# Keeping the activations of the last 16 expert blocks in SBUF between the hidden stage and the values stage

## The chip, the cores and the metric

One core of one Trainium2 chip runs the kernel. The metric is the device time of one execution in microseconds; the time before is the median of three runs. A profile is one execution recorded by the hardware profiler.

## The reference

A hybrid encoder layer is applied to a prompt of 512 tokens and a sample of 256 tokens: RMSNorm, one input projection, two attention mixers, the output projection with a residual, and then PEER, a layer of 128 x 128 = 16384 single-neuron experts. Only PEER matters here:

```python
def peer(h, w_q, sub_keys, u, v):
    ...
        best, pos = lax.top_k(cand, PEER_TOPK)
        eidx = jnp.take_along_axis(cand_idx, pos, axis=-1)
        g = jax.nn.softmax(best, axis=-1)
        act = jax.nn.gelu(jnp.einsum('cd,cpkd->cpk', xc, u[eidx]).astype(jnp.float32), approximate=False)
        return jnp.einsum('cpk,cpkd->cd', (g * act).astype(xc.dtype), v[eidx])
```

Each token picks 8 x 16 = 128 experts. Expert e contributes its gate times GELU(x . u[e]) times the row v[e].

## The kernel before

The 256 sample tokens fetch their experts by indirect DMA on POOL (`row`, L738: 128 rows of u and v, 1 MB, 256 of them), with the dot product and the sum on DVE (L740, L748). This goes on from the routing of the sample to nearly the end, beside everything else, paced by `early`, a list that names for each pair of dots the weight split after which they stand in DVE's order.

The 512 prompt tokens are done densely: all 16384 experts, in 128 blocks of 128, with a gate that is zero where a token did not pick an expert. Three stages do that.

*Hidden*: for block j, `hidden` (L601) loads 128 rows of u (`raw`, 0.5 MB, on SP), splits them into a high and a low part (`hi` on ACT, L72; `lo` on DVE, L73), runs 24 matmuls of 512 columns (`pu`, three for each of 8 chunks, L67 to L69), takes the GELU on ACT (`ge`, L608) and writes 256 KB to the DRAM tensor `h_d` (L609, issued by ACT). `raw` has three buffers. The first 16 blocks fill gaps of the routing; the others come after the gates in the program, but in fact run beside them.

*Gates*: one-hot matmuls (`pg`, L666) build the gate of each expert and token in 16 pieces (`gb`, 2 MB each), which are written to the DRAM tensor `g_d` (L670). Their pools, `gm` and `rq`, take much of SBUF, and are closed (`left.close()`, `rqx.close()`) behind the hidden loop.

*Values*: the pool `dense` (`dp`, 64 KB of each partition) is opened then, in the room that the gates had. For each pair of blocks jp, SP loads the hidden activations (`gw` from `h_d`, L699, three buffers) and for every fourth pair the gates of 8 blocks (`gblk` from `g_d`, L685, 2 MB, two buffers). DVE multiplies the two in place (L701), ACT and DVE split the product into `w` (which takes the buffers of `x2p`, the hidden matmuls' operand), the rows of v come as `raw` and are split like those of u, and 48 matmuls add to the 8 PSUM banks `py`. After the second pair the residual is loaded (`x1y`, four loads of 512 KB on SP, L712) and added through 64 matmuls with an identity (L715). At the end `py` is copied out.

Each engine runs its instructions in a fixed order, and so does each DMA queue. That order is worked out when the kernel is built, by a planner that goes by the order of the program, but takes a later instruction ahead where an earlier one isn't ready by its own timing. So a load of the values stage can stand in SP's queue among loads of the hidden stage, as soon as a buffer for it is free.

Of the kernel before, what the change touches and what calls it, by code (L numbers as in the profile page):

```python
# [11 lines left out]
F32 = mybir.dt.float32  # L12
F32R = mybir.dt.float32r
U32 = mybir.dt.uint32
BF = mybir.dt.bfloat16
AF = mybir.ActivationFunctionType
# [5 lines left out]
P = 128  # L22
D = 1024
# [7 lines left out]
NK = 128  # L31
# [7 lines left out]
DENSE = 4  # L39
# [5 lines left out]
NCAND = 64  # L45
FIRST_GATHER = 36
FILL = 16
NOSYNC = mybir.DependencyInfo(mybir.DependencyClass.NoSync, mybir.DependencyReason.DATA)


@with_exitstack
def tile_kernel(ctx, tc, xs_in, relb, onehot, logm, g1, w_in, gqk, lamv, gdiff, w_out, g2,
                w_q, skT, uT, uv, out_p, out_s, dbg=None):
    nc = tc.nc
    V, S, G, T = nc.vector, nc.scalar, nc.gpsimd, nc.tensor

    def f(ap):
        return ap.bitcast(F32)

    def pool(stack, name, bufs=1, side="left", **kw):  # L60
        return stack.enter_context(tc.tile_pool(name=name, bufs=bufs, side=side, reuse_waits="tile", **kw))

    def psum(stack, name, bufs):
        return stack.enter_context(tc.tile_pool(name=name, bufs=bufs, space=PSUM, reuse_waits="tile"))

    def mm3(ps, ah, al, bh, bl, start, stop):
        T.matmul(ps, ah, bh, start=start, stop=False)  # L67
        T.matmul(ps, ah, bl, start=False, stop=False)  # L68
        T.matmul(ps, al, bh, start=False, stop=stop)  # L69

    def split(hi, lo, raw, low=None):
        S.copy(hi, raw)  # L72
        return (low or G).tensor_tensor(lo, raw, f(hi), op=OP.subtract)  # L73
# [3 lines left out]
    late = pool(ctx, "late")  # L77
# [14 lines left out]
    right = ctx.enter_context(ExitStack())  # L92
    ppP = pool(right, "ppP", 3, side="right")

    def bank(p, name):
        return p.tile([P, 512], F32, tag="b", name=name)
# [442 lines left out]
    def wide(t):  # L539
        return t.rearrange("p (k a) n -> p k (a n)", k=2)  # L540

    def out_weights(d, nb, hi, lo):
        raw = wide(rw.tile([P, DC, P], F32, name="raw8", bufs=3))
        nc.sync.dma_start(raw, w_out[d * P:(d + 2) * P, nb * 512:(nb + 1) * 512].rearrange("(k p) n -> p k n", p=P))
        split(hi, lo, raw, G if d % 4 else V)
        return hi, lo

    ps = [bank(b, "pacc") for b in obanks]
    for d in range(0, DC, 2):
        wh, wl = out_weights(d, 0, *(wide(rw.tile([P, DC, P], F32R, name=k)) for k in ("hi8", "lo8")))  # L550
# [9 lines left out]
    for d in range(0, DC, 2):  # L560
        wh, wl = out_weights(d, 1, *(wo.tile([P, 2, 512], F32R, name=k) for k in ("woh", "wol")))
# [21 lines left out]
    right = ctx.enter_context(ExitStack())  # L583
    rp = pool(right, "rp", 1, side="right")

    def weights8(src):
        raw = rw.tile([P, DC, P], F32, name="raw8", bufs=3)
        nc.sync.dma_start(raw, src)
        hi = rw.tile([P, DC, P], F32R, name="hi8")
        lo = rw.tile([P, DC, P], F32R, name="lo8")  # L590
        return raw, hi, lo
# [6 lines left out]

    h_d = dram.tile([NK // 2, P, 2, 512], F32, name="h_d")

    def hidden(j, low):  # L601
        raw, hi, lo = weights8(uT[j])
        low_of[j] = split(hi, lo, raw, low)
        pu = bank((ps_o, ps_pl)[j % 2], "pu")
        for d in range(DC):
            mm3(pu, hi[:, d], lo[:, d], x2p[0][:, d], x2p[1][:, d], d == 0, d == DC - 1)
        ge = rw.tile([P, 512], F32, name="ge", bufs=3)
        S.activation(ge, pu, AF.Gelu)  # L608
        nc.scalar.dma_start(h_d[j // 2, :, j % 2], ge)  # L609

    low_of = {}
    route_keys(0, 4, x2p, rp, 2, prompt_weights, ps_mm, ps_sc2, lambda pz: hidden(pz, G))
    right.close()

# [29 lines left out]
    for t in range(DENSE):  # L644
# [3 lines left out]
        for tb in range(P // TB):  # L648
# [19 lines left out]
                    o = tq * TQ + c4 * 4  # L668
                    S.copy(gb[:, :, o:o + 4].rearrange("p j t -> p t j"), pg)  # L669
            nc.scalar.dma_start(g_d[t * (P // TB) + tb], gb)  # L670
    for j in range(FILL, NK):
        hidden(j, G if j < 20 else V)
    left.close()
    rqx.close()
    fps.close()


    ps_y = psum(ctx, "ps_y", 1)
    dp = pool(ctx, "dense", 2, side="right")
    py = [ps_y.tile([P, 512], F32, name=f"py{c}") for c in range(DC)]  # L680
    vrows = uv.rearrange("(i j) d -> j i d", j=NK)

    def gates(jb):
        gblk = dp.tile([P, DENSE * P // TB, JB, TB], F32, name="gblk")
        nc.sync.dma_start(gblk, g_d[:, :, jb * JB:(jb + 1) * JB, :].rearrange("b i j t -> i b j t"))  # L685
        return gblk

    def values_of(j):
        vr, vh, vl = weights8(vrows[j, :, D:].rearrange("i (c d) -> i c d", d=P))
        low_of[NK + j] = split(vh, vl, vr, V)  # L690
        return vh, vl

    for jp in range(NK // 2):
        jj = 2 * jp % JB
        wh, wl = (late.tile([P, 2, 2, 512], F32R, tag=f"x{i}", name=f"w{i}") for i in range(2)) if jp == 0 else (wh, wl)
        if jj == 0:
            gblk = gates(2 * jp // JB)
        ge = dp.tile([P, 2, 512], F32, name="gw", bufs=3)
        nc.sync.dma_start(ge, h_d[jp])  # L699
        ge4 = ge.rearrange("p k (b t) -> p k b t", t=TB)  # L700
        V.tensor_tensor(ge4, ge4, gblk[:, :, jj:jj + 2].rearrange("p b k t -> p k b t"), op=OP.mult)  # L701
        gh, gl = wh[:, jp % 2], wl[:, jp % 2]
        split(gh, gl, ge, V)
        vv = [values_of(2 * jp + k) for k in range(2)]
        for c in range(DC):
            for k, (vh, vl) in enumerate(vv):
                mm3(py[c], vh[:, c], vl[:, c], gh[:, k], gl[:, k],
                    jp == 0 and k == 0, jp == NK // 2 - 1 and k == 1)
        if jp == 1:
            x1y = dp.tile([P, DENSE, D], F32, name="x1y", bufs=1)  # L710
            for t in range(DENSE):
                nc.sync.dma_start(x1y[:, t], x1_d[t])  # L712
            for c in range(DC):
                for t in range(DENSE):
                    T.matmul(py[c][:, t * P:(t + 1) * P], x1y[:, t, c * P:(c + 1) * P], ident, start=False, stop=False)  # L715
# [13 lines left out]
    for t in (4, 5):  # L729
        acc = gp.tile([P, D], F32, name="acc")  # L730
        nc.sync.dma_start(acc, x1_d[t])
        for b in range(0, NPK, 2):
# [3 lines left out]
            for k in range(2):  # L736
# [4 lines left out]
                if k == 0:  # L741
                    after = early[(t - 4) * 64 + b // 2]
                    tc.add_manual_dep(dot.ins, after.ins.name, NOSYNC, reason="order")
                rows.append(r)
# [61 lines left out]
```

## Time and profile before

| | us |
|---|---|
| median of three runs | 2288.71 |
| lowest, highest | 2288.24, 2309.62 |
| the profiled execution | 2291.37 |
| its span | 2289.4 |
| PE busy with matmuls | 2156.3 |
| DVE busy | 1799.5 |
| ACT busy | 915.5 |

Times in the rows are counted from the start of the span. PE is the matmul engine, PEld its weight load, DVE the vector engine, ACT the scalar engine, POOL the one that issues the gathers, and SP the queue of most loads. A name like `raw<-in_uT_dram` says what is written from what. Idle time stands in brackets, with what ended it.

### The profile page before, as it was taken

To read this page: it belongs to the slowest core of one execution; us is meant where nothing else is said; L and a number is where in the kernel's file an instruction comes from. 1 tells how busy PE (TensorE), PEld (TensorE's weight loads), DVE (VectorE), ACT (ScalarE), POOL (GpSimd) and SP (SyncE) were. 2 spreads that over 40 slices of the span, in tenths; PEclk is the share of its full clock that TensorE was granted. 3 is DMA by queue.
4 is the path that set the end of the run, shared out by engine and by line. 5 is a ranking of instruction groups with operands and counts; after the bars stand their busy time and mean duration, and the time that the engine had idled before them with its cause. 6 is when DMAs were issued, how large, how long until landed. Compare 5 with 4: busy or idle time off the path is not lost.

```text
span 2289.4 us, 31065 instructions
## 1 busy us (share of the span) xinstructions
PE 2156.3 (94%) x11312; PEld 1774.7 (78%) x11312; DVE 1799.5 (79%) x3500; ACT 915.5 (40%) x1476; POOL 858.4 (37%) x626
## 2 busy tenths in 40 slices
PE   6999999957999989999999988999999999999998
PEld 4788789846787777878888876887788778888786
DVE  4645379996688999989999965666788878887786
ACT  4665587622332234545555532322233223323232
POOL 4767776623465632222423322221222322222221
PEclk9999999969999999999999998999999999999999
DMA  5534333314477776789899899897999999999985
GB/s 183 174 114 128 99 123 97 106 37 155 168 280 246 271 273 224 284 302 346 320 349 350 333 386 340 336 352 285 354 354 369 349 334 365 398 376 329 374 341 187
DMA packets 198553, 617.65 MB, mean 270 GB/s; under 512 B 15888, under 2 KB 82064, under 8 KB 163584
## 3 DMA queue, kind: packets, MB, share of 16 engines
q1 hardware_dynamic: 139840, 278.70, 35.1%
q0 software_dynamic: 36864, 268.45, 31.0%
q10 hardware_dynamic: 21696, 68.53, 7.8%
q8 instruction: 88, 1.44, 0.3%
q14 instruction: 65, 0.53, 0.1%
HBM read 542.17 MB, written 73.45 MB: 269 GB/s over the span
## 4 chain that ended last, share of the span: by engine, by line
PE 39%; issue 32%; DVE 11%; POOL 11%; DMA 5%; ACT 1%; SPq 0%; POOLq 0%; ACTq 0%; DVEq 0%
POOL row L738 9%; PE pu L69 5%; PE pu L67 5%; PE pu L68 5%; PE pacc L68 3%; PE pacc L69 3%; PE pacc L67 3%; DMA row<-in_uv_dram,eidx 3%; PE py L67 2%; PE py L68 2%; PE py L69 2%; PE pg L666 2%; PE pq L69 2%; PE pq L67 1%; PE pq L68 1%
## 5 line engine op out<-in xcount | busy, mean ns | idle before, releaser
L738 POOL DMA_INDIRECT row<-in_uv_dram,eidx x256 | 424.7, 1659 | 1147.8 <-DVE acc L748 1004.4
L72 ACT CAST hi<-raw 128x1024 fp32r<-128x1024 f32 x276 | 289.5, 1052 | 628.4 <-PE pu L68 223.7
L67 PE MATMUL pu<-x2p,hi 128*128 128x512 f32 x1024 | 408.4, 399 | 15.6 <-ACT hi L72 15.5
L69 PE MATMUL pu<-x2p,lo 128*128 128x512 f32 x1024 | 408.4, 399 | 12.7 <-DVE lo L73 10.6
L67 PE MATMUL py<-w,hi 128*128 128x512 f32 x1024 | 401.5, 394 | 16.0 <-ACT hi L72 13.6
L73 DVE TENSOR_TENSOR lo<-raw,hi 128x1024 fp32r<-128x1024 f32 x238 | 290.1, 1221 | 155.5 <-ACT hi L72 126.4
L68 PE MATMUL pu<-x2p,hi 128*128 128x512 f32 x1024 | 405.9, 396 | 0.0
L68 PE MATMUL py<-w,hi 128*128 128x512 f32 x1024 | 401.0, 392 | 0.0
L740 DVE CUSTOM_DVE_ANT_0 row<-row,st 128x1024 f32<-128x1024 f32 x256 | 330.2, 1295 | 62.0 <-DMA row<-in_uv_dram,eidx 61.8
L748 DVE SCALAR_TENSOR_TENSOR acc<-row,wgt,acc 128x1024 f32<-128x1024 f32 x256 | 328.9, 1285 | 5.5
L69 PE MATMUL py<-w,lo 128*128 128x512 f32 x1024 | 301.3, 390 | 2.8 <-DVE lo L73 2.8
L67 PEld LDWEIGHTS py<-w,hi 128*128 128x128 f32 x1024 | 193.6, 189 | 64.4 <-ACT hi L72 21.7
L67 PEld LDWEIGHTS pu<-x2p,hi 128*128 128x128 f32 x1024 | 195.0, 190 | 58.1 <-ACT hi L72 16.3
L69 PEld LDWEIGHTS pu<-x2p,lo 128*128 128x128 f32 x1024 | 194.5, 190 | 56.6 <-DVE lo L73 14.6
L69 PEld LDWEIGHTS py<-w,lo 128*128 128x128 f32 x1024 | 192.4, 188 | 43.5 <-DVE lo L73 3.7
L68 PEld LDWEIGHTS py<-w,hi 128*128 128x128 f32 x1024 | 193.8, 189 | 40.3 <-DVE w L73 0.3
L68 PEld LDWEIGHTS pu<-x2p,hi 128*128 128x128 f32 x1024 | 194.8, 190 | 38.6
L669 ACT COPY gb<-pg 128x512 f32<-128x512 f32 x128 | 132.6, 1145 | 78.5 <-PE pg L666 77.5
L73 POOL TENSOR_TENSOR wl<-wraw,wh 128x512 fp32r<-128x512 f32 x88 | 116.4, 1329 | 59.7 <-ACT wh L72 59.0
L72 ACT CAST w<-gw 128x1024 fp32r<-128x1024 f32 x64 | 67.1, 1050 | 151.7 <-PE py L69 151.0
L666 PE MATMUL pg<-og,oij 128*128 128x128 bf16 x1536 | 108.9, 220 | 4.2 <-DVE og L659 4.2
L745 ACT ACTIVATE wgt<-h 128x2 f32<-128x2 f32 x128 | 26.1, 204 | 212.0 <-DVE h L740 211.0
(309 smaller groups left out, 3666.7 us busy)
## 6 DMA issues: line engine op xcount, KB each, us to landing
raw<-in_uT_dram SPq DMA_DIRECT2D x128, 512.0 KB, 5.9
raw<-in_uv_dram SPq DMA_DIRECT2D x128, 512.0 KB, 7.9
h_d<-ge ACTq DMA_DIRECT2D x128, 256.0 KB, 5.6
g_d<-gb ACTq DMA_DIRECT2D x16, 2048.0 KB, 8.7
gblk<-g_d SPq DMA_DIRECT2D x16, 2048.0 KB, 17.2
gw<-h_d SPq DMA_DIRECT2D x64, 512.0 KB, 7.5
wraw<-in_w_in_dram SPq DMA_DIRECT2D x96, 256.0 KB, 2.8
toe<-bias_d SPq DMA_DIRECT2D x24, 448.0 KB, 4.2
```

The costliest lines, as they stand in the source:

```text
L67: T.matmul(ps, ah, bh, start=start, stop=False)
L68: T.matmul(ps, ah, bl, start=False, stop=False)
L69: T.matmul(ps, al, bh, start=False, stop=stop)
L72: S.copy(hi, raw)
L73: return (low or G).tensor_tensor(lo, raw, f(hi), op=OP.subtract)
L666: T.matmul(pg[:, c], oij[:, 0, c4 * 4 + c], og[k][:, c4 * 4 + c], start=k == 0, stop=k == 2)
L669: S.copy(gb[:, :, o:o + 4].rearrange("p j t -> p t j"), pg)
L738: G.indirect_dma_start(out=r, out_offset=None, in_=uv, in_offset=bass.IndirectOffsetOnAxis(ap=eidx[t][:, b + k:b + k + 1], axis=0))
L740: dot = V.tensor_tensor_reduce(r[:, :D], r[:, :D], x2r[t], 1.0, 0.0, OP.mult, OP.add, h[:, k:k + 1])
L745: S.activation(wgt, h, AF.Gelu)
L748: V.scalar_tensor_tensor(acc, rows[k][:, D:], wgt[:, k:k + 1], acc, op0=OP.mult, op1=OP.add)
```

## The change

GELU of blocks 112 to 127 is written to a tile `keep` in SBUF (16 x 512 floats, 32 KB of each partition) and not to `h_d`. The pool `dense` is opened ahead of the hidden loop, behind the closing of the gates' pools. The values stage begins with pairs 56 to 63, takes their activations from `keep`, and goes on with pairs 0 to 55, which load `gw` as before. `x1y` takes over the room of `keep` (same tag, one buffer) and is loaded and added after the eleventh pair in place of the second. The list that paces the sample's dots counts the value blocks by their new place.

```diff
+KEEP = 16
...
-    def hidden(j, low):
+    def hidden(j, low, own=None):
...
+        if own is not None:
+            S.activation(own, pu, AF.Gelu)
+            return
         ge = rw.tile([P, 512], F32, name="ge", bufs=3)
...
-    for j in range(FILL, NK):
-        hidden(j, G if j < 20 else V)
     left.close()
     rqx.close()
+    dp = pool(ctx, "dense", 2, side="right")
+    keep = dp.tile([P, KEEP, 512], F32, tag="keep", name="keep", bufs=1)
+    for j in range(FILL, NK):
+        hidden(j, G if j < 20 else V, keep[:, j - NK + KEEP] if j >= NK - KEEP else None)
     fps.close()
...
     ps_y = psum(ctx, "ps_y", 1)
-    dp = pool(ctx, "dense", 2, side="right")
...
-        low_of[NK + j] = split(vh, vl, vr, V)
+        low_of[NK + (j + KEEP) % NK] = split(vh, vl, vr, V)
...
-    for jp in range(NK // 2):
+    order = [*range((NK - KEEP) // 2, NK // 2), *range((NK - KEEP) // 2)]
+    for n, jp in enumerate(order):
...
-        ge = dp.tile([P, 2, 512], F32, name="gw", bufs=3)
-        nc.sync.dma_start(ge, h_d[jp])
+        if n < KEEP // 2:
+            ge = keep[:, 2 * n:2 * n + 2]
+        else:
+            ge = dp.tile([P, 2, 512], F32, name="gw", bufs=3)
+            nc.sync.dma_start(ge, h_d[jp])
...
-                    jp == 0 and k == 0, jp == NK // 2 - 1 and k == 1)
-        if jp == 1:
-            x1y = dp.tile([P, DENSE, D], F32, name="x1y", bufs=1)
+                    n == 0 and k == 0, n == NK // 2 - 1 and k == 1)
+        if n == KEEP // 2 + 2:
+            x1y = dp.tile([P, DENSE, D], F32, tag="keep", name="x1y", bufs=1)
             for t in range(DENSE):
                 nc.sync.dma_start(x1y[:, t], x1_d[t])
```

## Rows read from the trace of the kernel before

**Rows 1.** The page: busy us of the engines; GB/s in 40 slices of 57.2 us.

```profile
PE 2156.3 (94%) x11312; PEld 1774.7 (78%) x11312; DVE 1799.5 (79%) x3500; ACT 915.5 (40%) x1476; POOL 858.4 (37%) x626
GB/s 183 174 114 128 99 123 97 106 37 155 168 280 246 271 273 224 284 302 346 320 349 350 333 386 340 336 352 285 354 354 369 349 334 365 398 376 329 374 341 187
```

**Rows 2.** Windows: length, busy us and instructions by engine; PE's clock, DMA share, GB/s.

```profile
1340.00:1420.00 80.00, 63.11 (x255) 49.92 (x255) 41.91 (x52) 18.44 (x27) 17.48 (x11) 0.89 0.97 372
1420.00:1460.00 40.00, 40.00 (x178) 33.14 (x177) 26.25 (x33) 11.70 (x19) 8.56 (x7) 1.00 0.86 321
1460.00:1549.00 89.00, 87.04 (x385) 71.73 (x383) 57.92 (x69) 28.12 (x42) 22.24 (x16) 1.00 0.90 342
1549.00:1636.00 87.00, 83.33 (x389) 68.97 (x390) 61.98 (x72) 21.41 (x28) 18.60 (x12) 0.98 0.84 304
1636.00:2257.00 621.00, 607.85 (x2646) 497.11 (x2645) 512.56 (x588) 178.14 (x218) 166.08 (x104) 0.99 0.94 357
2257.00:2290.00 33.00, 23.60 (x105) 19.20 (x103) 13.84 (x16) 6.67 (x9) 0.00 (x0) 0.92 0.26 95
```

**Rows 3.** Timeline of PE: start, us, instructions, idle before them and its releaser.

```profile
1379.06 0.79 PE L67 MATMUL pu<-x2p,hi 128*128 128x512 f32 x1 [10.61 <-ACT hi L72]
1402.92 0.80 PE L67 MATMUL pu<-x2p,hi 128*128 128x512 f32 x1 [4.88 <-ACT hi L72]
1549.38 2.52 PE L67 MATMUL py<-w,hi 128*128 128x512 f32 x8 [2.34 <-ACT w L72]
1620.36 2.11 PE L69 MATMUL py<-w,lo 128*128 128x512 f32 x8 [2.78 <-DVE lo L73]
```

**Rows 4.** Waits of PE from 1549 to 2281, the greatest: total us, times, longest.

```profile
PE py L67 <- ACT hi L72: 13.6, 17, 2.9
```

**Rows 5.** Timeline of SP's queue and of ACT near 1358 us.

```profile
1358.13 0.38 SPq L685 DMA_DIRECT2D gblk<-g_d  x1
1358.56 7.83 SPq L699 DMA_DIRECT2D gw<-h_d  x2
1366.44 4.29 SPq L712 DMA_DIRECT2D x1y<-x_d  x4
1374.96 0.32 SPq L699 DMA_DIRECT2D gw<-h_d  x1
1376.30 0.33 SPq L588 DMA_DIRECT2D raw<-in_uT_dram  x1
1376.68 0.43 SPq L685 DMA_DIRECT2D gblk<-g_d  x1
...
1377.59 0.33 ACTq L609 DMA_DIRECT2D h_d<-ge  x1
1377.96 1.05 ACT L72 CAST hi<-raw 128x1024 fp32r<-128x1024 f32 x1 [14.32 <-DMA gw<-h_d]
```

**Rows 6.** Landing of raw loads: first of 1350 to 1420, then of 1420 to 1540.

```profile
DMA to landing us min/median/max: 5.7/14.0/21.5
...
DMA to landing us min/median/max: 3.6/8.3/9.1
```

**Rows 7.** Tiles ge (1455 to 1549), gw, x1y, row: ns min/median/max, first and last start.

```profile
L608 ACT ACTIVATE ge<-pu x18: 582/590/594, 1455.3 to 1547.8; 128x512 f32<-128x512 f32 x18
...
L701 DVE TENSOR_TENSOR gw<-gw,gblk x64: 1214/1219/1226, 1385.2 to 2242.1; 128x1024 f32<-128x1024 f32 x64
...
L715 PE MATMUL py<-ident,x1y x64: 272/275/275, 1573.4 to 1580.4; 128*128 128x128 f32 x64
...
L738 POOL DMA_INDIRECT row<-in_uv_dram,eidx x256: 933/1679/5755, 563.2 to 2248.3; - x128
```

**Rows 8.** Timeline of SP's queue and of DVE between 1557 and 1616 us.

```profile
1557.59 0.37 SPq L685 DMA_DIRECT2D gblk<-g_d  x1
1602.29 0.38 SPq L685 DMA_DIRECT2D gblk<-g_d  x1
...
1615.42 1.22 DVE L740 CUSTOM_DVE_ANT_0 row<-row,st 128x1024 f32<-128x1024 f32 x1 [7.82 <-DMA row<-in_uv_dram,eidx]
```

More of the change, by code (lines that the diff above doesn't have):

```diff
@@ L689, in values_of @@
         vr, vh, vl = weights8(vrows[j, :, D:].rearrange("i (c d) -> i c d", d=P))
-        low_of[NK + j] = split(vh, vl, vr, V)
+        low_of[NK + (j + KEEP) % NK] = split(vh, vl, vr, V)
         return vh, vl
-    for jp in range(NK // 2):
+    order = [*range((NK - KEEP) // 2, NK // 2), *range((NK - KEEP) // 2)]
+    for n, jp in enumerate(order):
         jj = 2 * jp % JB
-        wh, wl = (late.tile([P, 2, 2, 512], F32R, tag=f"x{i}", name=f"w{i}") for i in range(2)) if jp == 0 else (wh, wl)
+        wh, wl = (late.tile([P, 2, 2, 512], F32R, tag=f"x{i}", name=f"w{i}") for i in range(2)) if n == 0 else (wh, wl)
         if jj == 0:
             gblk = gates(2 * jp // JB)
-        ge = dp.tile([P, 2, 512], F32, name="gw", bufs=3)
-        nc.sync.dma_start(ge, h_d[jp])
+        if n < KEEP // 2:
[3 more added lines that the diff above has]
+            nc.sync.dma_start(ge, h_d[jp])
         ge4 = ge.rearrange("p k (b t) -> p k b t", t=TB)
```

## The prediction

> **What bounds the kernel now.** I read the page first: PE is busy 94% of the span, and in the second half the DMA engines move 285 to 398 GB/s almost to the end [rows 1]. So the question is which of the two sets the end where the change acts. The change acts from about 1340 us on: the last hidden blocks run to 1549 us, the values stage from there to 2280 us. The windows [rows 2] answer it by matmul counts. The stretch 1420 to 1460 runs without a gap: 178 matmuls in 40 us, 4.45 per us, at full clock. Against that rate:
> 1340 to 1420: 255 matmuls are worth 57.3 us, so 22.7 of 80 us are lost.
> 1549 to 1636 (the first 16 of the 128 values blocks): 389 matmuls, of which 64 are the short ones of x1y, done in 7.1 us (1573.4 to 1580.4, [rows 7]). (389 - 64) / 4.45 + 7.1 = 80.1, so 6.9 of 87 us are lost.
> 1636 to 2257: 2646 / 4.45 = 594.6, so 26.4 of 621 us are lost.
> Everything else is PE at its own pace; no saving of bytes shortens that. The change can win at most what lies in those losses, 56 us in all (2.4%), and only the part that the removed transfers cause.
>
> Next I looked at where PE stands still [rows 3]. Two gaps carry the first loss: 10.61 us before 1379.06 and 4.88 us before 1402.92, both waiting for a hi cast on ACT; the granted clock is 0.89 in that stretch, which together with short waits is the other 7 us. The values stage has 18.7 us of idle in 19 waits: 13.6 us in 17 for a cast of freshly loaded weights [rows 4], and 2.34 and 2.78 us [rows 3].
>
> The cause of the first loss stands in the queue of SP [rows 5]. At 1358 the gates are done, their room is free, and SP, whose next hidden weights still lack a buffer, issues what the values stage may already have: one gblk (2.1 MB), three gw (0.52 MB each), x1y (four loads of 0.52 MB), and after one raw a second gblk. That is 7.9 MB between 1358.1 and 1377.1, in front of the raw loads that the hidden blocks need. raw loads issued in this stretch take 14.0 us (median) to land, and 21.5 at most, against 8.3 us after it [rows 6]. ACT suffers with it: its h_d write was issued only at 1377.59, and the cast behind it on the in-order engine had waited 14.32 us for a gw landing [rows 5].
>
> **The change part by part.** *h_d writes of 16 blocks* go: 16 x 262 KB = 4.2 MB, and 16 issues of 0.33 us on ACT. They lie in 1461 to 1549. There PE is busy 87.0 of 89 us, and the 2 us it lacks are the hand-over at the end of it [rows 2, 3]. Worth nothing; PE's own work covers them. The GELU itself (0.59 us on ACT [rows 7]) stays, only its destination is another tile.
>
> *gw loads of 8 pairs* go: 8 x 0.52 = 4.2 MB out of 64 loads. Those the first 87 us of the values stage would issue are not there, since the three gw buffers are filled early and none comes free until pair n = 8 is split. *gblk's slots also come free earlier*: the product with the gates (1.22 us on DVE [rows 7]) for pair n can be made when GELU 2n+1 of the last sixteen is there, so the first slot is free after the fourth pair, about eight blocks of 5.4 us ahead of 1549, near 1505 us, and the second near 1549. Before, these reloads were issued at 1557.59 and 1602.29 [rows 8]. The second stood in the way: a gather row landed late, DVE stood 7.82 us in front of its dot product [rows 8], the lo behind it came late, and PE stood 2.78 us before 1620.36 [rows 3]. Of the 6.9 us lost here, the 2.34 us before 1549.38 [rows 3] are the hand-over (w sits in the buffers of x2p and needs the last hidden matmul), and stay, with some slow start. I take 3.5 us of gain, bounds 0 and 4.5.
>
> *The burst at 1358* loses x1y, since that tile now lies in the room of the kept blocks and can't be loaded before pair n = 7 is split. The two gblk and three gw stay (now of pairs n = 0 to 7 and n = 8 to 10): 5.8 MB instead of 7.9. At the 372 GB/s of that stretch [rows 2], 2.1 MB are 5.6 us. Bounds: nothing, if the first gap is set by gblk and gw alone (ACT's wait ended on a gw, not on x1y); and 22.7 us, the whole loss, if the rest then fits into the lead of three raw buffers. I take 5.6: the queue ahead of the next raw is shortened by that, and 5.8 MB in front of it are still a burst.
>
> *x1y* moves into the values stage: 2.1 MB, about 1615 to 1640, and its 64 matmuls (the same 7.1 us) to pair 10. A gblk is the nearest row, the same size: twelve of them lie in 1636 to 2257, where 26.4 us are lost from all causes, so 2.2 us each at most on the mean. I take +2; bounds 0 and 5. *gblk at 1505* meets the hidden blocks' raw loads, with the h_d writes gone. Nearest rows: 4.88 us of idle for a gblk on top of a burst, with the clock's share about 7; and the gblk of 1557.59, followed by no gap of note [rows 3, 8]. The second is nearer, as queues are short there: +1, bounds 0 and 7.
>
> *The order* of the blocks, the early-dot marks (counted by place in the sequence) and the number of matmuls, casts and dots stay the same: nothing. That the pool and the kept tile are made ahead of the hidden loop holds nothing back either: the gathers stand behind both in the program and run from 563 us on [rows 7]. If the kept tile were ordered as one piece, the first product would wait for the last GELU at 1548.4, some 2 to 3 us at the hand-over.
>
> Sum: -5.6 - 3.5 + 2 + 1 = -6.1 us. The profiled execution took 2291.4 us (span 2289.4), so 2285.3 by its own time; it stands 2.7 us above the median of the runs shown, 2288.7. By the median: 2282.6, about 2283 us.
>
> **The rivals.** *Nothing gained, or slightly lost.* The first gap stays because two gblk and three gw, packed closer than before, do the same to raw and to ACT; and the early gblk reloads near 1505 and 1549 each open a gap like that before 1402.92. Price: two times 7, less the 3.5 won: +10.5, so 2299 us. For it: ACT's wait ended on gw, which stays, and the second gblk now lies in the burst itself. Against: a lone gblk cost next to nothing at 1557.59. It decides from the point where a 2.1 MB load among raw loads takes longer than the buffers' lead, some 16 us (three blocks of 5.4); a median of 8.3 us leaves half of that.
>
> *The transfers were the bound.* 8.4 MB fewer at the 357 GB/s of 1636 to 2257 [rows 2] are 23.5 us: 2265 us. For it: a DMA share of 0.94 in that stretch. Against: PE loses only 26.4 of 621 us there, and the DMA engines fall to a share of 0.26 in the last 33 us with PE still going [rows 2]; the 4.2 MB of writes lie under a PE that loses nothing. [...]
>
> *The burst dissolves*: without x1y the raw loads get through in time, ACT's issue isn't held, and the whole 22.7 us come back: with -3.5 + 3, 2265 us.
>
> *A new stall inside the values stage*: x1y is issued on SP before the kept blocks are released, and the raw loads wait behind it in the same queue. To cost 1% (23 us) SP would have to stand over 39 us, as the lead of raw absorbs some 16; the order of DVE, which releases the kept tile, is fixed with SP's, so I see little for it: 2312 us or more.
>
> **How the numbers follow.** Forecast (2272 to 2288) 0.57; nothing gained or slightly lost (2288 to 2305) 0.23; transfers as the bound 0.05 and burst dissolved 0.09 (both about 2265, two thirds of it below 2266); new stall 0.06. The range from 2267 to 2301 leaves out the stall, two thirds of the two large gains, and the top of the small loss (0.04). The likeliest case's own range is 2272 to 2288. A change within 1% (2266 to 2312) is about what a measurement can't tell from none: 0.85. Faster by more than that 0.09, slower 0.06.
>
> **What would show it.** Right: SP issues two gblk and three gw near 1358 and no x1y; the PE gap near 1379 remains but is smaller, and the one near 1403 goes; a gblk near 1505 and x1y near 1615 to 1640; no gap over 1 us in the first 16 values blocks but the hand-over; hidden blocks 112 to 127 at the old pace of 5.4 us. Wrong: matmuls per us above 4.45 anywhere, or a gap over 3 us between 1500 and 1680, or the stretch after 1680 changed by more than 5 us, which nothing in the sum provides for.

## The result: 0.9% slower, and the profile after

| | before | changed |
|---|---|---|
| median of 11 runs each | 2291.99 us | 2312.37 us |
| lowest, highest | 2286.38, 2309.62 | 2307.59, 2323.89 |
| ratio, 95% interval | | 1.0088 (1.007 to 1.0105) |
| the profiled execution | 2291.37 us | 2323.89 us |

The change costs 20 us where 6 us of gain were forecast, and 2312 us lies outside the stated range. The profiled execution of the changed kernel was its slowest one. A second profile of it, from the first experiment, took 2309.65 us, near the median; sizes below are given from both where it matters.

The page of the changed kernel: span, and busy us by engine.

```profile
span 2322.1 us, 31013 instructions
PE 2175.4 (94%) x11312; PEld 1789.8 (77%) x11312; DVE 1799.8 (78%) x3500; ACT 914.0 (39%) x1476; POOL 863.0 (37%) x626
```

DVE, ACT and POOL are as busy as in [rows 1], to 5 us. PE has the same 11312 matmuls, but is busy 19.1 us longer (8.7 us in the second profile, 2165.0): its granted clock is 0.968 over the span, and 0.976 before. So of the 32.7 us by which this span is longer, more than half went into slower matmuls and the rest into standing still. Windows of the changed kernel (length, busy us and instructions of PE, PEld, DVE, ACT, POOL, then PE's clock, DMA share, GB/s): the 80 us behind the gates, the last hidden blocks, and the first eight pairs of the values stage, which are the kept ones.

```profile
1344.00:1424.00 80.00, 67.54 (x270) 53.61 (x268) 41.26 (x52) 19.24 (x29) 17.57 (x12) 0.89 0.96 353
1464.00:1555.50 91.50, 86.14 (x373) 70.56 (x371) 65.81 (x77) 26.66 (x40) 23.75 (x15) 0.98 0.81 307
1555.90:1664.60 108.70, 94.79 (x385) 75.94 (x386) 65.87 (x79) 24.39 (x32) 26.50 (x16) 0.94 0.68 252
```

The same eight pairs in the kernel before; its 448 matmuls hold the 64 short ones of x1y, 7.1 us.

```profile
1549.40:1649.50 100.10, 96.81 (x448) 80.13 (x449) 74.44 (x86) 24.72 (x31) 23.83 (x15) 0.98 0.86 314
```

The first stretch won: 270 matmuls against the 255 of [rows 2], worth 15 / 4.45 = 3.4 us. The second lost: 373 matmuls are worth 83.8 of 91.5 us, so 7.7 us are missing where the kernel before missed 89 - 385 / 4.45 = 2.5. The third is the loss that decides: 108.7 us against 100.1 - 7.1 = 93.0, so 15.7 us more (14.1 in the second profile, which took 107.1 us). PE stands still 10.6 us more there (13.9 of 108.7 us against 3.3 of 100.1), and the same matmuls take 5.1 us longer (94.8 us busy against 96.8 - 7.1 = 89.7), at a granted clock of 0.94 against 0.98. All that with DMA less busy than before, 252 GB/s against 314: the loads that the change took away are away. Outside these stretches the first profile is 4.2 us late at the end of the gates and loses 10.1 us behind pair 16; in the second profile these are 0.5 and 2.0 us.

Timeline of PE in the changed kernel: the gaps in these stretches that matter here, with their releaser.

```profile
1383.31 0.50 PE L68 MATMUL pu<-x2p,hi 128*128 128x512 f32 x1 [2.30 <-ACT hi L73]
1398.15 0.79 PE L68 MATMUL pu<-x2p,hi 128*128 128x512 f32 x1 [6.97 <-ACT hi L73]
1514.25 0.80 PE L70 MATMUL pu<-x2p,lo 128*128 128x512 f32 x1 [3.38 <-DVE lo L74]
1623.39 3.22 PE L70 MATMUL py<-w,lo 128*128 128x512 f32 x7 [3.37 <-DVE lo L74]
1637.53 1.88 PE L70 MATMUL py<-w,lo 128*128 128x512 f32 x7 [1.58 <-DVE lo L74]
1654.35 3.35 PE L70 MATMUL py<-w,lo 128*128 128x512 f32 x7 [5.65 <-DVE lo L74]
```

In the values stage before, PE waited mostly for hi on ACT [rows 4]. In the kept stretch it waits for lo on DVE. The long gaps cost more than their length here: behind those of 3.37 and 5.65 us seven matmuls take 3.22 and 3.35 us, behind that of 1.58 us 1.88. The granted clock is 0.58 from 1623 to 1627 us and 0.50 from 1654 to 1658, and 1.00 from 1637.5 to 1639.5, behind the short one. Who DVE waits for, over the whole span (total us, times, longest), first of the changed kernel, then of the kernel before:

```profile
DVE row L749 <- DMA row<-in_uv_dram,eidx: 114.4, 45, 9.4
```

```profile
DVE row L740 <- DMA row<-in_uv_dram,eidx: 61.8, 35, 8.1
```

The rows of the sample's gathers, which the change doesn't touch, arrive too late for DVE. In the kept stretch alone the wait is 32.4 us in 6 times, against 9.9 us in 2. They hardly travel longer: in the kept stretch they land 8.7 us (median) after their issue, 11.8 at most (9.7 and 10.2 in the second profile), against 8.9 and 13.8 in the first eight pairs before. They are asked for too late, or looked for too early. The timeline of DVE, and below it POOL, in one period of the kept stretch shows which:

```profile
1605.06 2.60 DVE L757 SCALAR_TENSOR_TENSOR acc<-row,wgt,acc 128x1024 f32<-128x1024 f32 x2
1607.58 2.35 DVE L74 TENSOR_TENSOR lo<-raw,hi 128x1024 fp32r<-128x1024 f32 x2
1609.85 1.22 DVE L749 CUSTOM_DVE_ANT_0 row<-row,st 128x1024 f32<-128x1024 f32 x1
...
1610.99 1.22 DVE L74 TENSOR_TENSOR w<-keep,w 128x1024 fp32r<-128x1024 f32 x1
1612.13 0.15 DVE L755 TENSOR_TENSOR wgt<-wgt,gate 128x2 f32<-128x2 f32 x1
1618.45 1.23 DVE L749 CUSTOM_DVE_ANT_0 row<-row,st 128x1024 f32<-128x1024 f32 x1 [6.17 <-DMA row<-in_uv_dram,eidx]
...
1619.60 2.60 DVE L757 SCALAR_TENSOR_TENSOR acc<-row,wgt,acc 128x1024 f32<-128x1024 f32 x2
...
1606.61 1.86 POOL L747 DMA_INDIRECT row<-in_uv_dram,eidx  x1 [11.34 <-DVE acc L757]
1608.78 1.97 POOL L747 DMA_INDIRECT row<-in_uv_dram,eidx  x1 [0.30 <-issue]
```

There are four row buffers, two pairs of rows. The sums at 1605.06 give a pair of buffers back, POOL issues the next two gathers at 1606.61 and 1608.78, and the second row is there at about 1618.4, some 13 us after those sums began. DVE has 7.2 us of work until then, those sums included, and the next thing in its order is a dot product of just that row. It stands 6.17 us. Behind it wait the sums of the pair whose dots are done, and with these sums the release of the next buffers. So the period is 1619.60 - 1605.06 = 14.5 us for one pair of rows, and DVE's order holds one pair of rows for each pair of blocks, which PE does in 48 / 4.45 = 10.8 us. The pattern repeats: waits of 2.2, 5.8, 6.2, 5.8 and 8.4 us follow each other, one for each pair of rows. In DVE's order in the changed kernel fifteen of pairs 63 to 83 of the gathers have a dot of the next pair ahead of their sums, seven of them among the eight pairs of the kept stretch; in the kernel before it is five, four of them in its first eight pairs of blocks. Only the first dot of a pair is held by the list that paces them, and the one that came ahead is the second.

DVE did not pass the waiting dot by: the hi that the first lo behind the sums takes was there at 1612.25 us (ACT's cast of 1611.21, 1.04 us), but this lo ran at 1622.12, right behind the sums, and PE stood 3.37 us for it, until 1623.39.

SP's queue in the changed kernel, for the loads whose place the prediction named:

```profile
1363.65 6.25 SPq L690 DMA_DIRECT2D gblk<-g_d  x2
1369.95 12.75 SPq L708 DMA_DIRECT2D gw<-h_d  x3
...
1515.36 0.38 SPq L690 DMA_DIRECT2D gblk<-g_d  x1
...
1559.09 0.38 SPq L690 DMA_DIRECT2D gblk<-g_d  x1
...
1640.96 1.85 SPq L721 DMA_DIRECT2D x1y<-x_d  x4
```

### The profile page after: what moved, and what is told of

Read it like the earlier page. It is cut to its first block, busy times and chain, and to the rows that moved or that the text cites. A ratio compares the mean times of both kernels' runs of the same rounds, so it can differ in the third digit from the quotient of the medians.

```text
span 2322.1 us, 31013 instructions
## 1 busy us (share of the span) xinstructions
PE 2175.4 (94%) x11312; PEld 1789.8 (77%) x11312; DVE 1799.8 (78%) x3500; ACT 914.0 (39%) x1476; POOL 863.0 (37%) x626
## 4 chain that ended last, share of the span: by engine, by line
PE 52%; issue 21%; DVE 11%; POOL 8%; DMA 7%; ACT 1%; ACTq 0%; POOLq 0%; SPq 0%; DVEq 0%
PE py L68 7%; PE py L69 7%; PE py L70 6%; POOL row L747 5%; PE pu L68 4%; PE pu L70 4%; PE pu L69 4%; DMA row<-in_uv_dram,eidx 3%; PE pacc L69 3%; PE pacc L70 3%; PE pacc L68 3%; DMA raw<-in_uv_dram 2%; PE pg L670 2%; PE pq L70 2%; PE pq L68 2%
## 5 line engine op out<-in xcount | busy, mean ns | idle before, releaser
L747 POOL DMA_INDIRECT row<-in_uv_dram,eidx x256 | 429.6, 1678 | 1174.6 <-DVE acc L757 1050.8
L70 PE MATMUL pu<-x2p,lo 128*128 128x512 f32 x1024 | 410.0, 401 | 18.3 <-DVE lo L74 14.5
L68 PE MATMUL py<-w,hi 128*128 128x512 f32 x1024 | 403.6, 396 | 17.8 <-ACT hi L73 15.5
L70 PE MATMUL py<-w,lo 128*128 128x512 f32 x1024 | 306.4, 396 | 16.8 <-DVE lo L74 16.8
L68 PEld LDWEIGHTS pu<-x2p,hi 128*128 128x128 f32 x1024 | 195.8, 191 | 52.0 <-ACT hi L73 10.1
L73 ACT CAST w<-gw 128x1024 fp32r<-128x1024 f32 x56 | 58.7, 1049 | 152.2 <-PE py L70 146.5
```

Of the source, the lines that this page charges most:

```text
L747: G.indirect_dma_start(out=r, out_offset=None, in_=uv, in_offset=bass.IndirectOffsetOnAxis(ap=eidx[t][:, b + k:b + k + 1], axis=0))
```

## The experiments

Theory A: the planner's order of DVE over the kept blocks, with dots ahead of sums, makes the loss. Rival B: the loads that moved (x1y, gblk) make it, and the late rows are their effect. All ratios are to the kernel before on the same chip, with 95% intervals.

| run | median us | ratio | first eight pairs, us without x1y | row waits of DVE in them, us |
|---|---|---|---|---|
| before | 2291.0, 2290.0, 2288.7 | 1 | 93.0 | 9.9 |
| changed, first profile | 2312.4 | 1.0088 (1.007 to 1.0105) | 108.7 | 32.4 |
| changed, again | 2309.65 | 1.0087 (1.0059 to 1.0115) | 107.1 | 28.2 |
| changed, all dots in order | 2280.1 | 0.9945 (0.9918 to 0.9972) | 90.3 | 0 |
| before, all dots in order | 2298.5 | 1.0031 (1.0007 to 1.0056) | 89.8 | 0 |
| block order only | 2285.4 | 0.9984 (0.9965 to 1.0003) | 89.9 | 4.6 |
| changed, late dots in order | 2275.7 | 0.9918 (0.989 to 0.9947) | 90.3 | 0 |
| the same again | 2273.8 | 0.9925 (0.9905 to 0.9946) | 90.3 | 0 |
| before, late dots in order | 2295.7 | 1.0019 (0.9996 to 1.0042) | 91.3 | 0 |
| before, x1y late, late dots in order | 2287.7 | 0.9976 (0.9952 to 1.0) | 100.9 | 0 |
| changed, products late | 2301.0 | 1.0043 (1.0017 to 1.0069) | 97.6 | 17.8 |
| before, dots put ahead | 2292.0 | 1.0003 (0.9986 to 1.002) | 93.9 | 13.5 |
| block order only, late dots in order | 2286.3 | 0.9978 (0.9954 to 1.0001) | 98.7 | 0 |
| 8 blocks kept, late dots in order | 2283.8 | 0.9981 (0.9962 to 1.0) | 90.9 | 0 |

The pairs are timed in one profiled execution each, from the first of 48 x 8 matmuls to the first behind them, less 7.1 us where x1y's matmuls lie among them.

**The changed kernel again.** No edit.

> The changed kernel once more, for a second profile beside the kernel before on this chip. Theory A (a late gather row stops DVE: in the order of DVE the second dot product of the next pair stands ahead of the sums of this pair, eight times in a row over the kept blocks): about 2312 us, ratio about 1.009; the waits of DVE for gather rows near 114 us again, with several of 5 to 8 us between 1556 and 1660. Rival B (the moved x1y load and the reloads of gblk): the same time, but the waits of DVE would be scattered differently, and the gaps of PE would lie behind x1y and gblk alone.

It came back as it was: 97.0 us of row waits in all, 28.2 of them in 5 times over the kept pairs.

**The dots in order.** The second dot of a pair is held behind the first, in the changed kernel and in the kernel before. No instruction and no load is added or taken away.

```diff
                 if k == 0:
                     after = early[(t - 4) * 64 + b // 2]
                     tc.add_manual_dep(dot.ins, after.ins.name, NOSYNC, reason="order")
+                    first = dot
+                else:
+                    tc.add_manual_dep(dot.ins, first.ins.name, NOSYNC, reason="order")
```

> The changed kernel with one more ordering: the second dot of a pair stays behind the first in DVE's order, so that no dot of the next pair stands ahead of the sums of this one over the kept blocks. All work and all loads are the same. Theory A: the waits of DVE for rows over the kept blocks go from 32 us to under 8, and 12 to 20 us come back: 2290 to 2300 us, ratio to before 0.998 to 1.004. Rival B (x1y and gblk loads make it slower): within 5 us of the changed kernel, 2307 to 2317.

> The kernel before with the same ordering of the dots. Theory A: it has one such long wait (7.8 us, with a gap of 2.8 us on PE) and few short ones, so it wins little: 2283 to 2292 us, ratio 0.995 to 1.0. If the ordering is worth something by itself and has nothing to do with the change, it wins as much here as in the changed kernel, 12 us or more: 2280 or below.

The changed kernel fell by 30 us, more than the 20 it had lost and more than was expected, and the row waits behind the gates are gone. Rival B is out as the cause of most of it: gblk and gw are loaded in the burst as before, gblk again at 1505.0 and 1550.1, x1y at 1621.3. Of the 29.3 us between the two profiles 16.8 lie in the kept pairs (107.1 to 90.3), 8.9 behind them, where the run before had 11.5 us of row waits, and 3.6 ahead of the values stage. The edit acts in the gates stage too: the last copy of gates comes at 1332.1 us against 1340.9 in the run before it. That is no gain in itself, as 57 hidden matmuls more are left behind it (868 against 811), worth 57 / 4.45 = 12.8 us. The kernel before moves in the same way (1329.7 against 1340.4 us, 868 matmuls against 811). Behind the gates it has gaps of 8.71 and 10.78 us in front of hidden blocks, and its values stage begins 4.0 us later than without the edit. It ended 0.3% slower, where a gain was expected: order of dots is not worth something everywhere.

**The same for late dots only**, from pair 56 on, so that the gates stage stays as it was:

```diff
-                else:
+                elif (t - 4) * 64 + b // 2 >= 56:
                     tc.add_manual_dep(dot.ins, first.ins.name, NOSYNC, reason="order")
```

> The changed kernel with the second dot held behind the first only from pair 56 on, which is from the last part of the hidden stage; the dots of the gates stage are left as they were, so their order can give nothing. Theory A: about 17 us come back over the kept blocks and about 4 in the last hidden blocks, against the changed kernel run earlier (2309.7): 2286 to 2294 us, ratio to before 0.997 to 1.001; no wait of DVE for a row over 1 us between the last hidden matmul and the ninth pair. If most of the gain of the run with all dots in order came from the gates stage: 2297 or more.

> The kernel before with the same ordering from pair 56 on. Theory A: it had 8 us of row waits in the last hidden blocks and 10 in the first values pairs, which cost PE about 3 us: 2284 to 2296 us. Its last hidden blocks may be 10 us slower or faster than that by how the burst of loads at 1358 us meets the raw loads, as in the run with all dots in order.

> The changed kernel with the late dots in order once more, for a second profile, since the first profiled execution was the slowest of its runs. Theory A: 2270 to 2284 us, ratio 0.989 to 0.996, no row wait over 1 us in the first eight values pairs; the gain over the kernel before with late dots in order should show in the stretch behind the kept blocks as fewer waits of ACT for raw.

The window of the kept pairs in the changed kernel with late dots in order, and below it one period of DVE:

```profile
1552.10:1642.40 90.30, 87.74 (x385) 72.00 (x385) 68.11 (x81) 24.12 (x31) 22.38 (x16) 1.00 0.82 306
```

```profile
1593.86 2.61 DVE L760 SCALAR_TENSOR_TENSOR acc<-row,wgt,acc 128x1024 f32<-128x1024 f32 x2
1598.40 1.23 DVE L74 TENSOR_TENSOR lo<-raw,hi 128x1024 fp32r<-128x1024 f32 x1 [1.93 <-PE py L70]
1599.98 1.23 DVE L74 TENSOR_TENSOR lo<-raw,hi 128x1024 fp32r<-128x1024 f32 x1 [0.36 <-ACT hi L73]
1601.12 1.22 DVE L749 CUSTOM_DVE_ANT_0 row<-row,st 128x1024 f32<-128x1024 f32 x1
...
1602.27 1.22 DVE L749 CUSTOM_DVE_ANT_0 row<-row,st 128x1024 f32<-128x1024 f32 x1
...
1603.41 1.22 DVE L74 TENSOR_TENSOR w<-keep,w 128x1024 fp32r<-128x1024 f32 x1
1604.55 0.15 DVE L758 TENSOR_TENSOR wgt<-wgt,gate 128x2 f32<-128x2 f32 x1
1604.74 2.61 DVE L760 SCALAR_TENSOR_TENSOR acc<-row,wgt,acc 128x1024 f32<-128x1024 f32 x2
```

The period is 1604.74 - 1593.86 = 10.9 us, PE's own. The buffers that the sums at 1593.86 free are looked for only after the next sums, 18 us later (1612.0), so a round of 13 us fits in. DVE now waits for PE (1.93 us), not PE for DVE. For the kept pairs this stands under theory A: 16.8 us come back. The gain over the changed kernel is 34 to 36 us in all, larger than the 20 expected; about 10 us of it lie behind the kept pairs, and theory A doesn't account for all of them. It is the version that beats both kernels, the one before by 0.75 to 0.8%. The kernel before with the same edit is 2295.7 us. So with the dots in order the change is worth 20 us, with its sign turned round.

The last hidden blocks did not recover. Blocks 112 to 127 took 89.5 us in the kernel before and 94.6 and 94.3 in the two profiles of the changed one; with late dots in order they take 93.3 and 96.4 (from their first matmul to the first of the values stage), though DVE waits for no row in them. Another load stops DVE in their place, and PE then stands 1.86 us before 1526.51 (3.66 in the second profile, where DVE's wait is 5.8 us). The timeline of DVE in the first profile:

```profile
1521.83 3.50 DVE L710 TENSOR_TENSOR gw<-gw,gblk 128x1024 f32<-128x1024 f32 x3 [4.01 <-DMA gblk<-g_d]
1525.24 1.22 DVE L74 TENSOR_TENSOR lo<-raw,hi 128x1024 fp32r<-128x1024 f32 x1
```

That gblk is the one that the prediction saw coming near 1505 us; here it is issued at 1507.0 and 1505.3. In the runs below that keep 8 blocks or none in the new order it is issued at 1549.9 us or later, and these blocks take 89.5 us.

**Only the order of the blocks**: the last 16 first, but written to memory and loaded again, x1y at its old place; once with the dots free and once with late dots in order.

```diff
-        hidden(j, G if j < 20 else V, keep[:, j - NK + KEEP] if j >= NK - KEEP else None)
+        hidden(j, G if j < 20 else V)
...
-        if n < KEEP // 2:
-            ge = keep[:, 2 * n:2 * n + 2]
-        else:
-            ge = dp.tile([P, 2, 512], F32, name="gw", bufs=3)
-            nc.sync.dma_start(ge, h_d[jp])
+        ge = dp.tile([P, 2, 512], F32, name="gw", bufs=3)
+        nc.sync.dma_start(ge, h_d[jp])
...
-        if n == KEEP // 2 + 2:
+        if n == 1:
```

> Only the order of the blocks is changed: the values stage begins with the last 16 blocks, but these still go to memory and come back (nothing is kept, x1y at its old place). Theory A: its order of DVE has two such places in the stage instead of nine, so it is near the kernel before: 2286 to 2298 us, ratio 0.998 to 1.003. A rival by which beginning with the last blocks costs in itself (their activations are written just ahead of being read): 2300 us or more.

> The new order of the blocks without keeping any, and the dots in order from pair 56 on. Beside the changed kernel with late dots in order (2275.7 us) it shows what the keeping alone is worth, and beside the kernel before with late dots in order (2295.7 us) what the block order alone is worth. By the prediction's terms the keeping is worth about 6 us less x1y's place: 2280 to 2284 us here if the block order gives the rest; 2290 to 2297 us if it is the keeping that gives all of the 20 us.

With dots free it is no slower than the kernel before, so beginning with the last blocks is not what costs. With late dots in order it lies between, 9 us below the kernel before with that edit and 11 to 13 above the changed one. The first eight pairs took 98.7 us in this execution with no row wait at all, against 90.3 with the blocks kept. That is one gap of 6.58 us of PE, for hi on ACT. It doesn't show that keeping the blocks gives 8 us there: with the dots free the same loads took 89.9 us, and the kernel before with late dots in order 91.3. What the keeping is worth can't be read from the medians alone either, as x1y leaves the burst with it: it is loaded early here, and late in the changed kernel.

**The products back in their stretch.** In the changed kernel the products of kept blocks and gates are made during the last hidden blocks; here those of pairs 3 to 7 are held back.

```diff
-        V.tensor_tensor(ge4, ge4, gblk[:, :, jj:jj + 2].rearrange("p b k t -> p k b t"), op=OP.mult)
+        prod = V.tensor_tensor(ge4, ge4, gblk[:, :, jj:jj + 2].rearrange("p b k t -> p k b t"), op=OP.mult)
+        if 3 <= n < KEEP // 2:
+            tc.add_manual_dep(prod.ins, low_of[NK + 2 * (n - 3)].ins.name, NOSYNC, reason="order")
```

> The changed kernel with the products of kept pairs 3 to 7 held back, each until a weight split three pairs ahead, so that DVE makes them in the values stage as the kernel before does; the dots are free. Theory A, second part (the planner puts dots ahead because the products have left this stretch of DVE): with the products back, its order has fewer dots ahead of the sums over the kept blocks, row waits there fall from 28 to 32 us to under 15, and 8 to 14 us come back: 2296 to 2303 us. If the products' place has nothing to do with it: within 4 us of the changed kernel, 2306 to 2314.

The time is in the range expected of theory A, and the kept pairs took 97.6 us, with 17.8 us of row waits (somewhat over the 15 expected):

```profile
1554.50:1652.10 97.60, 90.28 (x384) 72.49 (x385) 72.92 (x85) 24.62 (x31) 25.93 (x16) 0.98 0.79 293
```

DVE has more work between sums and dots again (72.9 us in 97.6 against 65.9 in 108.7), and fewer dots stand ahead: ten of pairs 63 to 83 against fifteen, four of eight in the kept stretch against seven. The products were taken out of the last hidden blocks, and there the row waits rose, from 21.8 us to 32.9 between the gates and the values stage; blocks 112 to 127 took 102.5 us against 94.3. This says that the departure of the products from a stretch carries a good part of the loss. It doesn't split that into less work between and another order.

**Dots put ahead in the kernel before.** For pairs 68 to 75 the sums are held behind the second dot of the next pair.

```diff
+            for k in (1, 0) if held else (0, 1):
...
+                elif held:
+                    for s_ in sums(*held):
+                        tc.add_manual_dep(s_.ins, dots[1].ins.name, NOSYNC, reason="order")
+                    held = None
...
+            if FLIP[0] <= pair < FLIP[1]:
+                held = rows, wgt
+            else:
+                sums(rows, wgt)
```

> The kernel before, with eight dots put ahead: for pairs 68 to 75 of the gathers, which fall into its first 16 values blocks, the sums stay behind the second dot of the next pair, as the changed kernel has it there. Nothing is kept, no load moves. Theory A: row waits of DVE in the first eight pairs rise from 10 us to 20 or more, and the time rises by 6 to 18 us: 2296 to 2309 us. If the late rows of the changed kernel come from its loads (x1y, gblk) and not from the order: within 4 us of the kernel before.

This expectation failed: no loss, and row waits of 13.5 us where 20 were expected, though every pair of the stretch has its sums behind a dot of the next. The timeline of DVE suggests why the same order costs little here:

```profile
1588.78 2.60 DVE L737 SCALAR_TENSOR_TENSOR acc<-row,wgt,acc 128x1024 f32<-128x1024 f32 x2
1591.30 1.22 DVE L702 TENSOR_TENSOR gw<-gw,gblk 128x1024 f32<-128x1024 f32 x1
1595.52 1.23 DVE L74 TENSOR_TENSOR lo<-raw,hi 128x1024 fp32r<-128x1024 f32 x1 [3.00 <-ACT hi L73]
1600.44 1.23 DVE L752 CUSTOM_DVE_ANT_0 row<-row,st 128x1024 f32<-128x1024 f32 x1 [3.70 <-DMA row<-in_uv_dram,eidx]
1601.60 1.22 DVE L74 TENSOR_TENSOR lo<-raw,hi 128x1024 fp32r<-128x1024 f32 x1
```

Between the sums and the dot lie 8.0 us of work and other waits, against 7.2 in the changed kernel, and of the two lo that a pair of blocks needs one runs ahead of the dot; no gap of PE follows the other one. The waits also don't come in every pair: three are over 2 us (4.08, 3.70 and 2.13), where the changed kernel has six. So theory A has to be narrowed: the order alone is not enough. It cost time where the waits followed each other pair after pair, with both lo behind the dot. That the missing products made the difference fits the run above, but no run holds the order fixed and changes the work between, so this part isn't shown.

**x1y late in the kernel before**, late dots in order.

```diff
-        if jp == 1:
+        if jp == 10:
             x1y = dp.tile([P, DENSE, D], F32, name="x1y", bufs=1)
```

> The kernel before with the residual loaded and added after the eleventh pair in place of the second, and the dots in order from pair 56 on; nothing is kept and the blocks have their old order. It takes x1y (2.1 MB) out of the burst of loads behind the gates. By the prediction's terms (burst 5.6 us shorter, x1y in the values stage 2 us): 3 to 6 us less than the kernel before with its late dots in order. If the gap behind the burst is set by gblk, gw and the wait of ACT: within 2 us of it.

The run doesn't test its question. The planner issued the load as early as its room allowed, still in the burst:

```profile
1360.65 10.70 SPq L699 DMA_DIRECT2D gw<-h_d  x3
1371.40 0.43 SPq L685 DMA_DIRECT2D gblk<-g_d  x1
1371.87 10.00 SPq L712 DMA_DIRECT2D x1y<-x_d  x3
```

In the changed kernel the room that it shares with the kept blocks holds it back. That the median here lies 8 us below the kernel before with late dots in order isn't explained. The profiled execution was the slowest of the run. Its first eight pairs took 100.9 us without a row wait: DVE stands up to 8.5 us for a gw load there, and PE 3.98 us for lo.

**Half as many kept.** KEEP = 8, late dots in order.

```diff
-KEEP = 16
+KEEP = 8
```

> Half as many blocks kept (8; x1y still in their room, after the seventh pair), late dots in order. If the gain grows with the bytes kept: half of the way between the kernel before with late dots in order (2295.7) and the changed one with them (2275.7), 2283 to 2289 us. If it comes from the new order or from x1y's place: 2273 to 2281 us, as with 16.

The time is where half of the gain would be, but it is no other than that of keeping none in the new order (0.9981 and 0.9978). So the points don't show that the gain grows with the bytes: from none kept to 8 the median falls by 2.5 us, within the intervals, and the other 8 to 10 us down to the changed kernel's 2273.8 and 2275.7 come between 8 and 16.

## Why the prediction was wrong

The step that failed is the one on order: "The order of the blocks, the early-dot marks (counted by place in the sequence) and the number of matmuls, casts and dots stay the same: nothing." The numbers did stay the same. The order on DVE didn't: the planner orders again around every edit, and it put second dots, which no mark holds, ahead of sums where the products had left. What it cost: 14.1 to 15.7 us over the kept pairs, a quarter to a third of it as slower matmuls at a lower granted clock (0.94 and 0.95 against 0.98), and 5 us in the last hidden blocks, where PE stood 3.38 us before 1514.25 (between the gates and the values stage DVE waited 22.0 us for rows, against 8.1). With dots in order the kept pairs take 90.3 us. So the step of the sum for this stretch, -3.5 us, measured 93.0 - 90.3 = 2.7 us against the kernel before, and 91.3 - 90.3 = 1.0 against it with the same edit, inside its bounds. (The window 1549 to 1636 holds 325 / 24 = 13.5 of the 16 blocks that the prediction names; over all sixteen the loss before was 100.1 - 7.1 - 384 / 4.45 = 6.7 us, so the term hardly moves.)

Point by point:

- *The writes to h_d, worth nothing.* The runs don't price them by themselves; the last hidden blocks became slower, for another reason.
- *The burst, -5.6 us.* Measured 3.4 us in the first profile and (274 - 255) / 4.45 = 4.3 in the second. SP did issue two gblk and three gw, and no x1y. The shape was wrong, though: the first gap shrank from 10.61 us [rows 3] to 2.30, and the one behind it grew from 4.88 to 6.97. It was said to go. ACT's wait there fell from 14.32 us [rows 5] to 6.00, now for a gblk.
- *x1y in the values stage, +2.* It was issued at 1640.96. Its price can be read only with the dots in order: pairs 8 to 16 took 95.4 - 7.1 = 88.3 us, against 87.8 before, so 0.5 us. In the changed kernel the wait of 8.44 us before the dot at 1649.41 falls on x1y's load and is the longest of the series. Its gather landed 11.8 us after its issue, the second gathers of the three pairs before it 9.1 to 9.5, so x1y may have added some 2.5 us to that one; this wasn't separated.
- *gblk in the hidden stage, +1.* Issued at 1515.36 in the changed kernel, and no gap follows it: nothing there. With late dots in order it shows: the last sixteen hidden blocks take 3.8 and 6.9 us more than before (93.3 and 96.4 against 89.5), inside the bounds of 0 to 7.
- *The hand-over* stayed at 2.34 us. In both profiles of the changed kernel 2.3 us more follow within 5 us, for w on DVE; the kernel before has no such gap.
- *The rivals.* The one on the slower side named a load issued ahead of its release on SP, and added that "the order of DVE, which releases the kept tile, is fixed with SP's". It was the order of DVE, but through the gathers. In the kept stretch SP waited 1.9 us to issue x1y, and ACT waited for no raw load: that the price of this rival, 2312 us or more, is the time that was measured is luck. The prediction had seen the pattern once: the 7.82 us wait [rows 8], which it put down to a gblk load alone. That load may have had its part: the gather that was issued 0.8 us before it took 13.8 us to land, against a median of 8.9. But the dot stood in front of sums that waited for nothing else, as in the series after. That transfers were the bound doesn't fit: the slowest stretch moved 252 GB/s, and 8.4 MB fewer brought no gain.
- *What was to show it wrong* did: a gap over 3 us between 1500 and 1680 us stands there three times. The stretch behind pair 16 changed by more than 5 us too, but in the first profile alone (10.1 us, 2.0 in the second).

What stays open: of the 20 us that the change is worth with late dots in order, the profiles place few. The first eight pairs differ by 1.0 us from those of the kernel before with that edit (91.3). In the stretch behind pair 16 the profiled executions took 535.6 and 536.6 us against 544.1, with as many loads, and there DVE's order differs too. This gain is not bound to the kept blocks: the new block order with nothing kept and late dots in order took 531.9 us there, the kernel before with x1y late 536.5. As the planner orders anew around each edit, a difference of this size between two versions can't be put down to the edit alone.

## What to carry to other kernels

Where a planner orders the queues, an edit that takes work from an engine can cost time there (14.1 to 15.7 us over the kept pairs here): ask which instruction of a chain that waits for late data (here a gather's row, 8.7 us after its issue) may now move ahead, and pin every member of such a chain, not only the first. Here a buffer that is freed by an instruction queued behind a wait for another refill of the same pool set a period of 14.5 us: the round from the freeing instruction to the landed row (some 13 us) plus the dot ahead of the next sums (1.2 us). That held with the DMA queues far from their fullest, at 252 GB/s against 398 in the fullest slice of the kernel before [rows 1]. And a gain predicted from loads should be measured a second time with the order of the side chain held, as its sign turned here.

## What the runs showed of the hardware

A gather's landing hardly followed the load in these stretches: it took 8.7 us (median) at 252 GB/s over the kept pairs (9.7 at 251 in the second profile) and 8.9 us at 314 GB/s in the kernel before. Fewer bytes on the queues did not bring the rows in earlier. The slowest in the first profile and in the kernel before, 11.8 and 13.8 us, were issued within 4 us of a load of 2.1 MB (x1y, gblk). And executions of one kernel spread by 9.8 to 25.3 us in the runs of seven or more (2266.7 to 2283.8 for the changed kernel with late dots in order), so that a profiled execution need not stand near its median.
